# Four edits to a hybrid GLA + RWKV-7 step: fewer x rows in waiting, state transposes ahead of projections, head sums as two fp32r products, and VectorE block transposes in place of TensorE's

## The chip, the cores and the metric

The kernel runs on one core of a Trainium2 chip. The metric is device microseconds (us) of one execution; lower is better. A few runs of the same kernel are shown by their median, and one further execution was recorded by the hardware profiler. The engines are called as the profile calls them: PE (TensorE matmuls), PEld (its weight loads), DVE (VectorE), ACT (ScalarE), POOL (GpSimd), SP (SyncE, which issues all DMAs here).

## The reference, cut to what matters

One layer of a decoder step, all in float32: 1024 prompt tokens and 8 sample tokens (with states of their own) go through one projection, two parallel recurrent branches, a gated merge and a layer norm.

```python
p = jnp.einsum('btd,dn->btn', x, w_in)                 # 1024 -> 3088 + 4224 + 2048 columns
q, k, v, g_a, a_lr = _split(p_gla, GLA_SPLITS)         # GLA: 4 heads, key 128, value 256
...
pr = p_rwkv + (prev - p_rwkv) * rwkv_mu                # token shift
r, kb, vb, g_b, w_lr, aa_lr = _split(pr, RWKV_SPLITS)  # RWKV-7: 16 heads of 64
kk = hr(kb * rwkv_k_k)
kk = kk / jnp.maximum(jnp.sqrt(jnp.sum(jnp.square(kk), axis=-1, keepdims=True)), L2_EPS)
...
# per token: S = S*w + (S·(-kk)) (kk*a)^T + v k^T ;  y = S r
y, S_rwkv = _rwkv7_scan(rh, hr(w), kh, vh, kk, hr(a), S_rwkv0)
mu = jnp.mean(y, axis=-1, keepdims=True)               # group norm per head
var = jnp.mean(jnp.square(y - mu), axis=-1, keepdims=True)
bonus = jnp.sum(rh * kh * rwkv_r_k, axis=-1, keepdims=True) * vh
...
m = sigmoid(gate_a) * (o_gla @ w_up_gla) + sigmoid(gate_b) * (o_rwkv @ w_up_rwkv)
y_out = _layernorm(DEEPNORM_ALPHA * x + m @ w_out, ln_g, ln_b, LN_EPS)
```

The outputs are the two y, and the new GLA, RWKV and shift states of both groups. Four sums over a head's 64 channels are taken per pair of heads: the one under `kk`, the one in `bonus`, and the mean and the variance of the group norm.

## The kernel before, in words

**Tiling.** Channels lie on the 128 partitions and tokens along the free dimension. The tokens go in two passes (`PASS`): pass 0 holds 512 prompt tokens and the 8 samples (two matmul tiles of 260), pass 1 the other 512. A block of the projection is 128 output columns: 8 steps over the 1024 inputs, and in each step three products of fp32r operands, `xh*whi`, `xl*whi`, `xh*wlo`, where hi is the value rounded to fp32r and lo is the rest. Per pass there are 73 blocks for `w_in`, then 8 for each of the two up projections, then the output projection. A weight row is split into hi and lo in pass 0, stored, and loaded again in pass 1.

**Order.** The kernel has no fixed loop order. Each piece of work is a Python generator (a stream) that yields one operation at a time; `Order.run` keeps a modelled time per engine, takes in each round the stream whose operation would start first, and issues it. Where two could start at the same time, a bonus by the kind of stream decides: `PRIO` on all engines but PE, `ON_PE` on PE. The projection blocks are one stream of kind "block" with bonus 0.0. The issued order is fixed when the kernel is built; on the chip each engine takes its instructions strictly in that order and waits at semaphores. Operations written through `self.C` may go to ACT or DVE, those through `self.E` to DVE or POOL, whichever ends first by the model.

**Buffers.** Tiles come from counted pools, and a stream that finds none waits: 26 `row` tiles of [128, 520], 4 `wide` of [128, 1024], 2 `part` (fp32r, for hi and lo of a sum's operand), 1 `sto`; in PSUM 2 banks `proj`, 3 `big`, 1 `pch`, 2 `pY`. The three `big` banks serve nearly everything beside the projections and the recurrent chain.

**A pair of RWKV heads** is one stream (`pair`), 8 pairs per pass, 16 in all. `front` makes decayed keys and values and the chunk matrices G (with two calls of `head_sums`), inverts 32x32 blocks by 31 DVE steps on the tiles `X` and `Xt`, with round trips through DRAM (`LD`, `XD`); `back` finishes the 64x64 inverses; `turn` makes the keys `BK` and the values `v` token-major; `chain` runs over the 8 chunks of 64 tokens one after the other, and a pair's chain starts only when the chain of the pair before has ended; `norm` (two more calls of `head_sums`) finishes. In pass 1 `chain` spawns `state`, a stream of kind "state" that takes a `big` bank, transposes the final state `Sp` on PE, copies it to `sto` and stores it (`rwkv_p`). The samples' streams (`rwkv_sample`, `tails`) are of kind "state" too.

**Head sums** are one float32 matmul of a [128, 512] row with a block matrix of ones (`heads`, part of the constants `cons`). **`turn`** transposes 8 chunks of `BK` [128, 128] and 4 blocks of `v` on PE through three `big` banks and copies them back: 2 copies of 128x512 and 4 of 64x256 per pair. The tile `L` of the inversion is used again for the values.

**`load_x`** loads the 8 rows of the next matmul's moving operand (x, the branch outputs or the merged rows) into `row` tiles; two helper streams split each into `xh` and `xl`, for which there is one buffer per step, free only when the last block that reads the old one is done. `swap` starts it 3 blocks early (`AHEAD`). For x itself, `low_rank` also multiplies the raw rows, three at a time.

Of the kernel before, what the change touches and what calls it, by code (L numbers as in the profile page):

```python
# [11 lines left out]
F32R = mybir.dt.float32r  # L12
# [8 lines left out]
P = 128  # L21
# [5 lines left out]
HT = TP // 2  # L27

PASS = [(0, HT + NS, NS, [(0, 260), (260, 260)]), (HT + NS, HT, 0, [(0, 512)])]
GH, GDK, GDV = 4, 128, 256  # L30
RH, RN = 16, 64
NPAIR = RH // 2
C = 64
NCH = HT // C
# [21 lines left out]

KEEP = 1
AHEAD = 3
SPARE_ROWS = 8


# [12 lines left out]
PRIO = {"evacuate": 0.7, "pair": 0.4, "turn": 0.5, "chain": 0.5, "norm": 0.1, "x": 0.7, "lora": 0.2, "rank": -0.3,  # L74
        "head": 0.3, "gate": 0.05, "w": 0.3, "out": -0.1, "state": 0, "block": 0.0}
ON_PE = {"evacuate": 0.0, "pair": 0.15, "turn": 0.1, "chain": 0.15, "norm": 0.15, "x": 0.0, "lora": 0.15, "rank": 0.1,
         "head": 0.1, "gate": 0.06, "w": 0.0, "out": -0.03, "state": 0.0, "block": 0.0}

URGENT = 0.6
SIGMOID, EXP = "sigmoid_and_others", "natural_log_exp_and_others"  # L80
# [2 lines left out]
HS = (slice(0, 64), slice(64, 128))  # L83
# [7 lines left out]

CST = {}
_o = 0
for _n, _w in [("ident", 128), ("gmask", 256), ("heads", 128)]:
    CST[_n] = (_o, _w)
    _o += _w
CST_W = _o
# [9 lines left out]
def constants():  # L107
    c = np.zeros((P, CST_W), np.float32)

    def put(name, v):  # L110
        o, w = CST[name]
        c[:, o:o + w] = v

    i = np.arange(P)
    put("ident", np.eye(P))
    put("heads", (i[:, None] // C) == (i[None] // C))
    s, t = i[:, None] % C, i[None, :] % C
    put("gmask", np.concatenate([s < t, s <= t], axis=1))
    lev = np.zeros((P, 64 * MASKED), np.float32)
    for n, m in enumerate(LEVELS[:MASKED]):  # L120
        ri = np.array([x for x in range(P) if (x // m) % 2 == 1])
        j = i[:, None]
        lev[:, 64 * n:64 * n + 64] = ((j // (2 * m)) == (ri[None, :] // (2 * m))) & ((j // m) % 2 == 0)
    return c, lev


class Op:
# [274 lines left out]
class Kern(Order):  # L402
# [57 lines left out]

    def head_sums(self, x):

        ps = yield from self.bank("big", [P, HT])
        yield self.P.matmul(ps, self.cst("heads"), x, start=True, stop=True)
        return ps

    def pvec(self, name, j):
# [4 lines left out]
    def setup(self):  # L472
        nc, a = self.nc, self.a
        E = mybir.EngineType
        self.es.enter_context(self.tc.manual_schedule(engines={E.PE, E.Activation, E.DVE, E.Pool, E.SP}))
        cp = self.pool("const")
        wp = self.pool("w", side="left")
        self.dr = self.pool("dr", space=DRAM)
        pp = self.pool("psum", space=PSUM)
        xp = self.pool("x", side="right")  # L480
        self.r1 = r1 = self.pool("work", side="left")
        for tag, bufs in BANKS.items():
            self.buffers(tag, bufs, lambda tag=tag, bufs=bufs: pp.tile([P, 512], F32, name=tag, bufs=bufs))
        for tag, (shape, bufs) in SBUF.items():
            dt = F32R if tag in PARTS else F32
            self.buffers(tag, bufs, lambda tag=tag, shape=shape, bufs=bufs, dt=dt:
                         r1.tile(shape, dt, name=tag, bufs=bufs))
        for tag, (shape, bufs) in WBUF.items():
            dt = F32 if tag == "wraw" else F32R
            self.buffers(tag, bufs, lambda tag=tag, shape=shape, bufs=bufs, dt=dt:  # L490
                         wp.tile(shape, dt, name=tag, bufs=bufs))
        for k in range(NK):
            for v in "hl":
                tag = f"x{v}{k}"
                self.buffers(tag, 1, lambda tag=tag: xp.tile([P, HALF], F32R, name=tag, bufs=1))
        nc.scalar.preload_act_table_set(EXP)
        self.cons = cp.tile([P, CST_W], F32, name="cons")
        self.pv = cp.tile([P, PV_W], F32, name="pv")
        self.ident = self.cst("ident")
        self.omu = cp.tile([P, NRC], F32, name="omu")  # L500
        self.oka = cp.tile([P, 8], F32, name="oka")
        self.nkk = cp.tile([P, 8], F32, name="nkk")
        self.bias = {}
        for n, v in [("glaeps", GLA_EPS), ("gneps", GN_EPS), ("lneps", LN_EPS), ("one", 1.0),
                     ("kkl", 0.5 * math.log(KK_SCALE))]:
            t = cp.tile([P, 1], F32, name="b_" + n)
            nc.vector.memset(t, v)
            self.bias[n] = t
        dbg = getattr(self, "dbg", {})
        self.o_gla = dbg.get("o_gla", None) or self.dr.tile([D, T], F32, name="o_gla")  # L510
        self.o_rwkv = dbg.get("o_rwkv", None) or self.dr.tile([D, T], F32, name="o_rwkv")
        self.sg = [[[self.dr.tile([P, PASS[i][1]], F32, name=f"sg{i}{n}{k}") for k in range(NK)] for n in range(2)]
                   for i in range(2)]
        self.mg = [[self.dr.tile([P, PASS[i][1]], F32, name=f"mg{i}{k}") for k in range(NK)] for i in range(2)]

        self.lev = cp.tile([P, 64 * MASKED], F32, name="lev")

        self.onesr = cp.tile([P, P], F32R, name="onesr")
        self.wa = cp.tile([P, NK * 16], F32, name="wa")
        self.alr = [cp.tile([96, HALF], F32R, name=f"alr{n}") for n in range(2)]  # L520
        self.gw2 = cp.tile([96, GH * GDK], F32R, name="gw2")
        self.GS = [cp.tile([P, GDV], F32, name=f"GS{h}") for h in range(GH)]

        self.smp = cp.tile([P, 4, NPAIR, NS], F32, name="smp")
        self.RS = self.dr.tile([4, NS, D], F32, name="RS")
        self.WA = self.dr.tile([2, NS, D], F32, name="WA")
        self.tail = cp.tile([P, NS + 1, NRC], F32, name="tail")
        self.carry = cp.tile([P, NRC], F32, name="carry")
        self.shT = cp.tile([P, NRC, NS], F32, name="shT")
        self.reset = cp.tile([P, HT], U8, name="reset")  # L530
        nc.vector.memset(self.reset, 1)
        nc.vector.memset(self.reset[:, ::C], 0)

        self.Sp = [cp.tile([P, C], F32, name=f"Sp{n}") for n in range(NPAIR)]
        for t in self.Sp:
            nc.gpsimd.memset(t, 0.0)

        for tag, n, bufs in (("az", 4 * HT, 2), ("XT", 2 * HT, 2), ("X1", HT, 1), ("As", 2 * HT, 1)):
            ts = [cp.tile([P, n], F32, name=f"{tag}{i}") for i in range(bufs)]
            for t in ts:  # L540
                nc.gpsimd.memset(t, 0.0)
            self.fixed(tag, ts)
# [9 lines left out]
    def load_constants(self):  # L552
        a, V, E = self.a, self.V, self.E
        yield from self.load("wa", self.S.dma_start(self.wa, a["wa"]))
        self.has.add("wa")
        row = yield from self.row()
# [13 lines left out]
        yield V.tensor_scalar(self.nkk, self.pv[:, o:o + 8], -1.0, None, ALU.mult)  # L570
        self.has.add("pv")
        yield from self.load("cst", self.S.dma_start(self.cons, a["cst"]))
        raw = row[0:96, :GH * GDK]
        for n in range(3):
            yield self.S.dma_start(raw[32 * n:32 * n + 16], a["gla_alpha_w2"])
        yield self.S.dma_start(self.lev, a["lev"])
        yield V.tensor_copy(self.gw2, raw)
        yield V.tensor_sub(self.gw2[64:96], raw[64:96], self.gw2[64:96].bitcast(F32))
        self.free(row)
        self.has.add("cst")  # L580


    def load_x(self, src, i, wait=None, low_rank=False):
# [3 lines left out]
        base, n = PASS[i][:2]  # L587
        raws, his, xs, used = [], [], [], [NK]
# [20 lines left out]
        self.spawn(high(), "x")  # L609
        self.spawn(low(), "x")  # L610
        for k in range(NK):
            raw = yield from self.row(n)
            rows = slice(k * P, (k + 1) * P)
            yield from self.load(f"x{k}", self.S.dma_start(
                raw, src[k] if isinstance(src, list) else src[rows, base:base + n]))
            raws.append(raw)
# [540 lines left out]

    def turn(self, d):

        for x in range(0, NCH, 4):  # L1160
            pt = yield from self.bank("big", [P, 4, P])
            for n in range(4):
                yield self.tr(pt[:, n], d.BK[:, x + n])
            yield self.C.copy(d.BK[:, x:x + 4], pt)
            self.free(pt)
        d.u = d.L.rearrange("p (c h v) -> p c h v", c=NCH, h=2)
        pt = yield from self.bank("big", [P, 4, P])
        for n in range(4):
            yield self.tr(pt[:, n], d.v[:, n * P:(n + 1) * P])
        self.free(d.v)  # L1170
        for h in range(2):
            for n, hs in enumerate(HS):
                yield self.C.copy(d.u[HS[1 - h], n::2, h], pt[hs, :, h * C:h * C + C])
        self.free(pt)

    def chain(self, c, p, d):
        A, V = self.A, self.V
# [335 lines left out]
    def swap(self, src, i, wait=None, low_rank=False):  # L1513

        if self.plan:
            self.plan[-1].last = True
        self.todo = (max(0, len(self.plan) - AHEAD), (src, i, wait, low_rank))

# [94 lines left out]

def layout(i):
    f = np.ascontiguousarray
    cst, lev = constants()
    ch = lambda v: v.reshape(-1, P).T
    pv = np.concatenate([ch(i["rwkv_mu"][0]), ch(i["rwkv_w0"][0]), ch(i["rwkv_a0"][0]), ch(i["rwkv_k_k"][0]),
                         ch(i["rwkv_k_a"][0]), ch(i["rwkv_r_k"][0].reshape(-1)), ch(i["rwkv_lnx_w"][0]),
# [2 lines left out]
    x = np.concatenate([xp, xs], axis=0)  # L1622
    xT = f(np.concatenate([xp[:HT], xs, xp[HT:]], axis=0).T)
    return {
        "cst": cst, "lev": lev, "pv": f(pv), "xT": xT, "x": f(x), "w_in": f(i["w_in"][0]),
        "wa": f(i["w_in"][0][:, OFF_A:OFF_R].reshape(NK, P, 16).transpose(1, 0, 2).reshape(P, NK * 16)),
        "gla_alpha_w2": f(i["gla_alpha_w2"][0]), "state_gla": f(i["state_gla"]), "state_rwkv": f(i["state_rwkv"]),
        "shiftT": f(i["state_rwkv_shift"][0].reshape(NS, NRC, P).transpose(2, 1, 0)),
# [25 lines left out]
```

## Time and profile before

| | |
|---|---|
| median of 3 runs | 1686.61 us (1685.98 to 1691.09) |
| profiled execution | 1687.94 us, span of the trace 1686.2 us |
| granted TensorE clock, mean | 0.986 |
| busy share PE / PEld / DVE / ACT / POOL | 97% / 85% / 70% / 49% / 5% |
| DMA | 315.26 MB, 187 GB/s over the span |

A busy PE is not a PE at its peak: a matmul's record includes the time until its result lands, so the records of neighbours overlap (a 128x512 fp32r product has a record of 0.40 us and starts 0.23 us after the one before). The granted clock of a stretch stands as PEclk. Nearly all instructions are recorded under one line, L214, the helper that issues them; groups are therefore told apart by their tiles.

### The profile page before, as it was taken

The page shows a single profiled execution, that of the slowest core. Times are in us where ns is not written, and L with a number is a line of the kernel's source. Part 1 is how long each engine was busy: PE and PEld are TensorE (multiplying, and loading weights), DVE is VectorE, ACT ScalarE, POOL GpSimd, SP SyncE. Part 2 cuts the span into 40 slices and gives each one's busy share as a digit, 9 for nine tenths or more (in the row PEclk, how much of TensorE's full clock was granted, in tenths as well). Part 3 has the DMA queues.
Part 4 walks back from the last instruction along what each step waited for, and adds up shares of the span by engine and source line. Part 5 has one row for each costly group of instructions (what it writes and reads, how often), then busy time and mean ns, then how long its engine had stood idle before and what let it go on. Part 6 is the DMA issues. An engine that isn't in the chain of part 4 may idle for free.

```text
span 1686.2 us, 29927 instructions
## 1 busy us (share of the span) xinstructions
PE 1628.7 (97%) x10322; PEld 1430.9 (85%) x10322; DVE 1184.6 (70%) x3114; ACT 830.7 (49%) x1974; POOL 86.0 (5%) x183
## 2 busy tenths in 40 slices
PE   8999999999999998999999999999989999999998
PEld 7899999999999996888878778778867889988786
DVE  6777876887688766757656477898728876656565
ACT  5456755664657465443634254526243656644210
POOL 1100000100000000000000000200000000000000
PEclk9999999999999999899999999999988999999999
DMA  9777675777587657545364625454642487788522
GB/s 291 246 228 231 217 215 152 227 246 218 160 245 228 216 158 237 170 119 174 101 206 123 186 73 176 152 163 156 202 145 67 114 275 221 236 278 278 182 78 87
DMA packets 311778, 315.26 MB, mean 187 GB/s; under 512 B 75347, under 2 KB 197084, under 8 KB 311628
## 3 DMA queue, kind: packets, MB, share of 16 engines
q1 hardware_dynamic: 311628, 313.36, 59.9%
q8 instruction: 82, 1.34, 0.3%
q14 instruction: 68, 0.56, 0.1%
HBM read 195.45 MB, written 117.82 MB: 186 GB/s over the span
## 4 chain that ended last, share of the span: by engine, by line
PE 73%; DVE 12%; DMA 7%; ACT 3%; issue 2%; SPq 2%; POOL 0%; POOLq 0%; DVEq 0%; ACTq 0%
PE proj L214 41%; PE big L214 21%; PE pY L214 7%; DVE row L214 4%; PE pch L214 4%; DMA wide<-LD 2%; SPq L214 2%; DVE X L214 2%; DVE Xt L214 2%; ACT row L214 1%; DVE wide L214 1%; DMA row<-state_rwkv 1%; DVE wlo L214 1%; DVE az L214 1%; DMA wraw<-w_up_gla 1%
## 5 line engine op out<-in xcount | busy, mean ns | idle before, releaser
L214 PE MATMUL proj<-xl,whi 128*128 128x260 f32 (+1 forms) x1928 | 637.5, 331 | 0.0
L214 PE MATMUL proj<-xh,whi 128*128 128x260 f32 (+1 forms) x1928 | 635.9, 330 | 0.0
L214 PE MATMUL proj<-xh,wlo 128*128 128x260 f32 (+1 forms) x1928 | 635.0, 329 | 0.0
L214 PEld LDWEIGHTS proj<-xh,wlo 128*128 128x128 f32 x1928 | 364.9, 189 | 29.9 <-issue 6.6
L214 PEld LDWEIGHTS proj<-xh,whi 128*128 128x128 f32 x1928 | 365.2, 189 | 28.5 <-issue 5.4
L214 PEld LDWEIGHTS proj<-xl,whi 128*128 128x128 f32 x1928 | 364.9, 189 | 28.6 <-issue 6.5
L214 DVE TENSOR_TENSOR row<-row 128x256 f32<-128x256 f32 (+6 forms) x326 | 161.7, 503 | 23.8 <-ACT row L214 11.8
L214 ACT CAST whi<-wraw 128x512 fp32r<-128x512 f32 x210 | 129.9, 622 | 95.7 <-PE proj L214 51.7
L214 DVE TENSOR_TENSOR wlo<-wraw,whi 128x512 fp32r<-128x512 f32 x205 | 141.0, 691 | 40.5 <-ACT whi L214 37.3
L214 ACT ACTIVATE row<-row 128x512 f32<-128x512 f32 (+4 forms) x229 | 138.4, 611 | 44.6 <-DVE row L214 26.3
L214 DVE TENSOR_TENSOR Xt<-X,wide 128x60 f32<-128x60 f32 (+24 forms) x496 | 105.4, 212 | 43.8 <-DMA wide<-LD 31.2
L214 ACT ACTIVATE row<-proj,omu 128x260 f32<-128x260 f32 (+1 forms) x99 | 54.1, 547 | 150.2 <-PE proj L214 149.9
L214 PE MATMUL big<-row 128*128 128x64 f32 (+4 forms) x712 | 115.6, 282 | 12.5 <-DVE row L214 11.5
L214 PEld LDWEIGHTS big<-row 128*128 128x128 f32 (+1 forms) x712 | 96.9, 193 | 23.3 <-DVE row L214 13.5
L214 ACT ACTIVATE s0p<-wide,pc 64x64 f32<-64x64 f32 x256 | 88.1, 344 | 52.7 <-DVE wide L214 48.5
L214 DVE TENSOR_TENSOR X<-X,Xt 128x60 f32<-128x60 f32 (+24 forms) x496 | 104.8, 211 | 11.9
L214 ACT COPY wide<-pch 64x64 f32<-64x64 f32 x221 | 45.5, 206 | 114.3 <-PE pch L214 110.4
L214 DVE SCALAR_TENSOR_TENSOR row<-proj,pv,row 128x259 f32<-128x259 f32 (+1 forms) x99 | 56.3, 569 | 49.7 <-ACT tail L214 33.7
L214 DVE SCALAR_TENSOR_TENSOR wide<-pch,pc,s0p 64x64 f32<-64x64 f32 x224 | 63.1, 282 | 38.3 <-PE pch L214 33.7
L214 POOL TENSOR_TENSOR row<-row 128x512 f32<-128x512 f32 (+7 forms) x43 | 45.5, 1059 | 794.4 <-ACT row L214 211.7
L214 ACT COPY row<-big 128x128 f32<-128x128 f32 (+7 forms) x165 | 46.7, 307 | 66.8 <-PE big L214 63.5
L381 ACT ACT_TABLE_LOAD x56 | 71.8, 1283 | 1.0
(254 smaller groups left out, 2560.6 us busy)
## 6 DMA issues: line engine op xcount, KB each, us to landing
wraw<-w_in SPq DMA_DIRECT2D x146, 256.0 KB
wh<-whi SPq DMA_DIRECT2D x146, 256.0 KB
wl<-wlo SPq DMA_DIRECT2D x146, 256.0 KB
whi<-wh SPq DMA_DIRECT2D x146, 256.0 KB
wlo<-wl SPq DMA_DIRECT2D x146, 256.0 KB
wide<-LD SPq DMA_DIRECT2D x64, 128.0 KB
wraw<-w_up_gla SPq DMA_DIRECT2D x32, 256.0 KB
wraw<-w_up_rwkv SPq DMA_DIRECT2D x32, 256.0 KB
```

The costliest lines, as they stand in the source:

```text
L214: ways.append((eng, lambda call=call: call(out, *args, **kw), price(eng, name, out, args, ins)))
L381: self.nc.scalar.preload_act_table_set(self.table)
```

## The change

Four edits, independent of each other in the code:

1. `load_x`: the load of row k is held back until fewer than 4 loaded rows wait for their split (`RAWS`), except for the first x.
2. `ON_PE["state"]` goes from 0.0 to 0.1, so that PE operations of the "state" streams are taken ahead of projection products that could start at the same time.
3. `head_sums`: the operand is split into hi and lo (one rounding copy on ACT or DVE, one subtraction on DVE or POOL), and two fp32r products with an fp32r block matrix `headsr` are summed in PSUM in place of one float32 product. The block matrix is loaded by a DMA of its own and cast once.
4. `turn`: no PE transposes. DVE transposes the 32x32 blocks of `BK` (into `L`) and of `v` (into a new `row`), and 16 + 8 copies of [32 partitions x 256], on ACT or DVE, put the blocks in their places. `L` is freed after the copies, and the values take another `wide` tile.

```diff
+RAWS = 4
...
-         "head": 0.1, "gate": 0.06, "w": 0.0, "out": -0.03, "state": 0.0, "block": 0.0}
+         "head": 0.1, "gate": 0.06, "w": 0.0, "out": -0.03, "state": 0.1, "block": 0.0}
...
     def head_sums(self, x):
 
+        hi, lo = yield from self.split(x)
         ps = yield from self.bank("big", [P, HT])
-        yield self.P.matmul(ps, self.cst("heads"), x, start=True, stop=True)
+        yield from self.sums(ps, self.headsr, hi, lo)
+        self.free(hi, lo)
         return ps
...
+        self.headsr = cp.tile([P, P], F32R, name="headsr")
...
-        raw = row[0:96, :GH * GDK]
+        raw, heads = row[0:96, :GH * GDK], (yield from self.row(P))
+        yield self.S.dma_start(heads, a["heads"])
...
+        yield V.tensor_copy(self.headsr, heads)
...
         for k in range(NK):
+            yield lambda: k - len(his) < RAWS or low_rank and not i
             raw = yield from self.row(n)
...
     def turn(self, d):
 
-        for x in range(0, NCH, 4):
-            pt = yield from self.bank("big", [P, 4, P])
-            for n in range(4):
-                yield self.tr(pt[:, n], d.BK[:, x + n])
-            yield self.C.copy(d.BK[:, x:x + 4], pt)
-            self.free(pt)
-        d.u = d.L.rearrange("p (c h v) -> p c h v", c=NCH, h=2)
-        pt = yield from self.bank("big", [P, 4, P])
-        for n in range(4):
-            yield self.tr(pt[:, n], d.v[:, n * P:(n + 1) * P])
+        q = [slice(32 * n, 32 * n + 32) for n in range(4)]
+        t, tv_ = d.L.rearrange("p (c j f) -> p c j f", c=NCH, j=4), (yield from self.row(HT))
+        yield self.V.transpose(d.L, d.BK.rearrange("p c t -> p (c t)"))
+        yield self.V.transpose(tv_, d.v[:, :HT])
         self.free(d.v)
+        for i in range(4):
+            for j in range(4):
+                yield self.C.copy(d.BK[q[j], :, q[i]], t[q[i], :, j])
+        self.free(d.L)
+        u = yield from self.get("wide")
+        d.u = u.rearrange("p (c h v) -> p c h v", c=NCH, h=2)
+        tv = tv_.rearrange("p (c j f) -> p c j f", c=NCH, j=2)
         for h in range(2):
-            for n, hs in enumerate(HS):
-                yield self.C.copy(d.u[HS[1 - h], n::2, h], pt[hs, :, h * C:h * C + C])
-        self.free(pt)
+            for i in range(2):
+                for j in range(2):
+                    yield self.C.copy(d.u[q[2 - 2 * h + j], :, h, q[i]], tv[q[2 * h + i], :, j])
+        self.free(tv_)
```

More of the change, by code (lines that the diff above doesn't have):

```diff
@@ L93 @@
 _o = 0
-for _n, _w in [("ident", 128), ("gmask", 256), ("heads", 128)]:
+for _n, _w in [("ident", 128), ("gmask", 256)]:
     CST[_n] = (_o, _w)
@@ L115, in constants @@
     put("ident", np.eye(P))
-    put("heads", (i[:, None] // C) == (i[None] // C))
     s, t = i[:, None] % C, i[None, :] % C
@@ L123, in constants @@
         lev[:, 64 * n:64 * n + 64] = ((j // (2 * m)) == (ri[None, :] // (2 * m))) & ((j // m) % 2 == 0)
-    return c, lev
+    return c, lev, ((i[:, None] // C) == (i[None] // C)).astype(np.float32)
 class Op:
@@ L578, in load_constants @@
         yield V.tensor_sub(self.gw2[64:96], raw[64:96], self.gw2[64:96].bitcast(F32))
-        self.free(row)
+        yield V.tensor_copy(self.headsr, heads)
+        self.free(row, heads)
         self.has.add("cst")
@@ L1615, in layout @@
     f = np.ascontiguousarray
-    cst, lev = constants()
+    cst, lev, heads = constants()
     ch = lambda v: v.reshape(-1, P).T
@@ L1624, in layout @@
     return {
-        "cst": cst, "lev": lev, "pv": f(pv), "xT": xT, "x": f(x), "w_in": f(i["w_in"][0]),
+        "cst": cst, "lev": lev, "heads": heads, "pv": f(pv), "xT": xT, "x": f(x), "w_in": f(i["w_in"][0]),
         "wa": f(i["w_in"][0][:, OFF_A:OFF_R].reshape(NK, P, 16).transpose(1, 0, 2).reshape(P, NK * 16)),
```

## The prediction

> **What bounds the kernel now.** I read the page's busy shares first, then what PE waits for, then stage windows (us of PE, PEld, DVE, ACT, POOL, then granted clock, DMA share, GB/s), then the chain that ended last and PE's timeline where the windows looked odd.
>
> ```profile
> PE 1628.7 (97%) x10322; PEld 1430.9 (85%) x10322; DVE 1184.6 (70%) x3114; ACT 830.7 (49%) x1974; POOL 86.0 (5%) x183
> PE big L214 <- DVE row L214: 13.4, 11, 5.5
> PE pch L214 <- DVE rh L214: 6.5, 10, 1.4
> 0.00:1391.00 1391.00, 1345.60 (x8731) 1187.68 (x8732) 1010.14 (x2799) 721.48 (x1759) 83.25 (x180) 0.98 0.60 185
> 1391.00:1686.00 295.00, 283.08 (x1593) 243.23 (x1592) 174.46 (x316) 109.25 (x215) 2.77 (x3) 0.99 0.60 194
> ```
>
> PE is busy 97%, and its longest sum of waits on one releaser is 13.4 us: PE bounds the kernel nearly everywhere, so work taken off PE should show. The second row of windows is the tail of up and output projections. All pairs' DVE work but little is in the first 1391 us, where DVE is at 1010.14/1391 = 73%.
>
> ```profile
> 632.00:716.00 84.00, 76.44 (x468) 64.35 (x467) 59.90 (x155) 42.66 (x97) 3.92 (x13) 0.92 0.66 205
> 935.00:1000.00 65.00, 59.78 (x288) 48.59 (x286) 37.13 (x89) 24.52 (x56) 4.00 (x9) 0.92 0.44 130
> 1000.00:1188.00 188.00, 183.78 (x1004) 153.22 (x1004) 154.75 (x409) 90.91 (x225) 20.58 (x28) 1.00 0.51 157
> 1238.00:1306.00 68.00, 59.21 (x302) 47.46 (x300) 44.67 (x128) 29.75 (x79) 2.99 (x9) 0.85 0.26 74
> ```
>
> Three stretches of pass 1 lose PE time, in gaps and by a lowered clock; 1000:1188 beside them shows the usual state (2.2% idle, clock 1.00). Ahead of two of them the chain of waits has nothing but projections for 27 and 50 us:
>
> ```profile
> 935.08 27.42 PE proj L214 x118
> 1187.97 50.17 PE proj L214 x216
> 1188.00:1238.00 50.00, 0.04 (x1) 0.15 (x2) 0.69 (x1) 0.00 (x0) 1.00 0.73 226
> 1237.96 0.49 PE L214 MATMUL big<-cons,Sp 128*64 128x128 f32 x3
> L214 PE MATMUL big<-cons,Sp x8: 270/271/273, 962.4 to 1579.7; 128*64 128x128 f32 x8
> ```
>
> The third row counts only operations on `big` banks: none in 50 us of pass 1. What ends it is three transposes of `Sp` in a row. `state` takes its bank before it asks for PE, and its bonus of 0.0 ties with the projections, which are in the list before it; so three finished pairs sit on all three `big` banks, and front, back, turn, norm and GLA can't get one until the projections run dry. When the banks come free, PE has few projections left to fill with, and the gaps follow.
>
> **The clock.** The wait of 5.5 us is at 670.7, and the clock behind it is 0.50:
>
> ```profile
> 676.22 1.02 PE L214 MATMUL big<-row 128*128 128x8 f32 x4 [5.49 <-DVE row L214]
> 678.00:682.00 4.00, 3.13 (x14) 2.94 (x15) 3.62 (x16) 0.26 (x3) 0.00 (x0) 0.50 0.30 102
> 1241.00:1245.00 4.00, 3.07 (x14) 2.74 (x14) 0.83 (x2) 0.97 (x3) 0.00 (x0) 0.70 0.21 67
> 1245.00:1249.00 4.00, 2.39 (x11) 1.80 (x10) 0.69 (x1) 2.67 (x5) 0.00 (x0) 0.50 0.00 0
> ```
>
> So a gap costs itself and some microseconds at half clock behind it. The Trainium skill, "TensorE: Matmul & The Clock Gate", section "Part 1: The HAM clock gate", says that an idle window of about 3.4 us halves the clock; the first two rows agree, while in the last two PE is idle 0.9 and 1.6 us of 4 and the clock falls all the same, so density counts as well as the longest gap.
>
> **Part 1: head sums.** 16 pairs x 4 = 64.
>
> ```profile
> 730.62 1.02 PE L214 MATMUL big<-row,cons 128*128 128x512 f32 x2
> L214 PE MATMUL big<-row,cons x128: 590/592/1167, 47.9 to 1461.4; 128*128 128x512 f32 x128
> 700.83 0.40 PE L214 MATMUL proj<-xl,whi 128*128 128x512 f32 x1
> 701.06 0.40 PE L214 MATMUL proj<-xh,wlo 128*128 128x512 f32 x1
> L214 DVE CAST part<-row x5: 420/426/429, 683.9 to 1319.0; 128x512 fp32r<-128x512 f32 x4, 128x520 fp32r<-128x520 f32 x1
> L214 ACT CAST part<-row x5: 615/628/642, 172.9 to 1561.3; 128x520 fp32r<-128x520 f32 x3, 128x512 fp32r<-128x512 f32 x2
> L214 DVE TENSOR_TENSOR part<-row,part x8: 684/690/694, 174.4 to 1319.7; 128x520 fp32r<-128x520 f32 x4, 128x512 fp32r<-128x512 f32 x4
> ```
>
> A float32 product is two records (128 for 64); the pair spans 1.02, one lasts 0.59, so the second starts 0.43 after the first, and a head sum holds PE for 0.86 us. fp32r products follow each other by 0.23, so two hold it for 0.46. PE: 64 x 0.40 = -25.6 us. Added: 64 casts (0.43 on DVE or 0.63 on ACT) and 64 subtractions (0.69 on DVE), and about 1.2 us of latency per sum inside a pair's stream.
>
> **Part 2: turn.** 12 PE transposes per pair, 192 in all.
>
> ```profile
> 717.38 0.60 PE L214 MATMUL big<-cons,wide 128*128 128x128 f32 x4
> 717.82 0.60 PE L214 MATMUL big<-cons,row 128*128 128x128 f32 x4
> L214 ACT COPY wide<-big 64x256 f32<-64x256 f32 x61 | 22.4, 367 | 3.5 <-PE big L214 2.2 <-DVE wide L214 0.5
> L214 ACT COPY wide<-big 128x512 f32<-128x512 f32 x27 | 15.8, 586 | 11.5 <-PE big L214 11.2
> L214 DVE STREAM_TRANSPOSE row<-row 128x512 f32<-128x512 f32 x16 | 11.3, 704 | 0.0
> L214 DVE CAST l2p<-l2s x12: 284/294/296, 44.0 to 1318.8; 128x256 fp32r<-128x256 f32 x12
> L214 ACT CAST l2p<-l2s x4: 405/406/426, 117.1 to 813.6; 128x256 fp32r<-128x256 f32 x4
> ```
>
> Four transposes take 0.44, so 0.11 each: PE -192 x 0.11 = -21.1 us. Removed on ACT (mostly): 2 x 0.59 + 4 x 0.37 = 2.6 us per pair. Added on DVE: one transpose of 512 (0.70) and one of 1024 (twice, 1.41): 2.1. Added on either: 24 copies of 256 elements a partition. No row has them with 32 partitions from SBUF; the casts of 256 are nearest, 0.29 on DVE and 0.41 on ACT. Bounds: all on DVE 24 x 0.29 = 7.1 us per pair, all on ACT 9.8. The turn gets some 5 us longer; PE fills with projections meanwhile, so I cost that latency at nothing in the sum; for the last pair the cover is the up projections, and if the cover is gone it is 5 us per pair (fourth rival).
>
> The Trainium skill speaks against this part: "VectorE: DVE Perf Modes", section "Rules for kernel authors", sends a 128x128 transpose to TensorE where PSUM will do. In engine time the rows agree with it: 12 x 0.11 + 2.6 = 3.9 us before against 9 to 12 us after. It would be the better way if PE had room, and PE has none; how that could turn the sign is the third rival.
>
> **Part 3: state transposes first.** The eight transposes cost the same; the banks come free at once. At stake are 65 - 59.78 = 5.2 and 68 - 59.21 = 8.8 us of gaps, and 8% of 65 and 15% of 68 = 15.4 us of clock: up to -29. The usual 2.2% idle stays (-3), and the refilled order has waits of its own; I take -20, between 0 (the banks are held by others then) and -26. By the code SP gains too: a store that waits for the one `sto` tile holds up all issues behind it, and three no longer come at once.
>
> **Part 4: few x rows.**
>
> ```profile
> 651.05 2.46 SPq L214 DMA_DIRECT2D row<-xT  x5
> L214 ACT CAST xh<-row x8: 613/617/624, 693.4 to 697.1; 128x512 fp32r<-128x512 f32 x8
> 2.11 4.32 DMA row<-xT
> ```
>
> Pass 1's eight rows are issued by 655 and split only at 693: 8 of 26 rows lie idle 40 us. Four come free, which can help the stretch 632:716 (7.6 us of gaps, 8% of clock: at most -14); but its 5.49 us wait is a sample matmul behind a DMA, not a missing row, so I take 0. The cost: a swap's fifth row may be issued late. A flight of 4.3 us against four steps of three products (4 x 0.69 = 2.8) leaves 1.5 us, over the 7 later swaps at most +11; I take 0, since a row issued in time has its 3 blocks of lead as before. On SP the issues only move later. The `heads` DMA at the start takes 64 KB that `cons` loses: 0.
>
> **What DVE and ACT pay.** Per pair DVE gets 2.1 + 4 x 0.69 = 4.9 us for certain (78 us in all), and up to 4 x 0.43 + 7.1 = 8.8 more (219 in all, if nothing goes to ACT). With PE's 46.7 us and the 20 of part 3 gone, the first 1391 us become 1324, and DVE's share 1088/1324 = 82% to 1229/1324 = 93%. How full can DVE be with PE still fed?
>
> ```profile
> 505.00:548.00 43.00, 42.93 (x345) 41.33 (x345) 37.26 (x93) 31.88 (x75) 1.42 (x2) 1.00 0.73 229
> 1096.00:1138.00 42.00, 39.91 (x222) 33.31 (x221) 38.21 (x115) 11.73 (x32) 1.91 (x2) 1.00 0.54 163
> ```
>
> At 87% PE was full; at 91% it lost 2 us in 42. The middle (1159 us) is at 87.5%, just there. If 87% is the ceiling, the middle costs 1159/0.87 - 1324 = +8, the upper end +89. ACT has room (52% there), and the model sends copies to it when DVE is late, so I stay near the middle and take +20, with 0 and +89 as ends.
>
> **The sum**, against the profiled execution (1687.94, which is 1686.2 of span and 1.7 around it): -25.6 - 21.1 - 20 + 0 + 20 = -46.7, so 1641. The median shown is 1.3 lower: 1640.
>
> **The rivals.**
> - All of it lands: -25.6 - 21.1 - 26 - 14, no DVE cost: 1601. For it: ACT half idle, POOL idle. Against: DVE at 82% at best.
> - The banks were not the cause, or the stall moves: the "state" bonus gives 0, and the rest stays: 1661. Against: the three `Sp` in a row end it.
> - Slower, by one mechanism: DVE becomes the bound in the pair stage. DVE takes all 24 copies and casts, 1229 us, and can't be kept above 87%: 1413 us of stage against 1391, +22, so 1709. It turns the sign where the ceiling is under 1229/1391 = 88%. For it: the copies change partition block each time, and the rows above lose PE time at 91%. Against: the planner counts DVE's time and can use ACT.
> - PE's time comes back as waits: the order is made anew, the streams in it are serial, and a quarter of the 10 us of added latency per pair (5 in turn, 4 x 1.2 in the sums) shows as PE gaps with half clock behind them: 16 x 2.5 = +40, 1681. For it: the 5.5 us wait shows that the planner's times can be off. Against: PE's waits inside the chain are short now (6.5 us in 10).
>
> **How the numbers follow.** Sum 0.45 (own range 1622 to 1658), all lands 0.18, banks not the cause 0.12, given back 0.13, DVE-bound 0.12. From no change a measurement can tell about 0.3%, 5 us, so 1682 to 1692 is "same". Faster: 0.45 + 0.18 + 0.12 + 0.05 of the "given back" = 0.80; same 0.07; slower 0.13. The range leaves out the slow case and the edge of the fast one: 1603 to 1690.
>
> **What would show it.** Right: no `Sp` transposes in threes, no 50 us of pure projections, the clock above 0.99; `big<-part,headsr` records of 0.39 instead of 0.59; PE's matmul count down by 192; DVE busy 1260 to 1400 with PE still at 96%. Wrong: PE under 93% with long waits on DVE block copies (`wide<-wide`), block copies far above 0.3 us, or new gaps of over 3 us with 0.50 behind them. At swaps, waits of PE on `row<-xT`, `row<-o_gla` or `row<-mg` would show part 4 as a cost.

## The result, and the profile after

The changed kernel takes 1634.97 us (median of four runs, 1634.04 to 1635.56); the kernel before takes 1687.66 us (four runs, 1685.98 to 1691.09). The ratio is 0.9685, with a 95% interval of 0.9668 to 0.9702, so 52.7 us are gained where 46.7 were forecast. The profiled execution took 1634.97 us with a span of 1633.0.

First the busy shares and the clock by slices, from the page of the changed kernel, then its two stage windows (us of PE, PEld, DVE, ACT, POOL, then granted clock, DMA share, GB/s):

```profile
PE 1580.9 (97%) x10130; PEld 1404.8 (86%) x10130; DVE 1309.8 (80%) x3396; ACT 880.3 (54%) x2112; POOL 116.0 (7%) x204
PEclk9999999899999999999999999999999999999999
```

```profile
0.00:1391.00 1391.00, 1347.86 (x8935) 1208.97 (x8936) 1165.45 (x3153) 799.98 (x1960) 111.98 (x200) 0.99 0.63 194
1391.00:1633.00 242.00, 233.01 (x1197) 195.79 (x1196) 144.30 (x244) 80.31 (x152) 4.06 (x4) 0.99 0.58 188
```

The matmul count is down by 192, DVE is up by 125 us, and PE is still busy 97%. Only one slice of the 40, that from 286 to 327 us, has a clock under 0.9. Both first windows end at 1391 us, so the gain shows in the second row: pass 1 has got further by then, and the tail is 242 us instead of 295.

A split of the span that is used throughout: idle PE time (span less busy), clock loss (one less the granted clock, times the span), and the rest, which is PE's work at full clock. Idle time at half clock is counted in both of the first two, so the three are good to a few us only. Before it is 57.5 + 23.6 + 1605; after, 52.1 + 18.0 + 1563. PE's work fell by 42 us, idle time by 5, clock loss by 6.

The stretches that the prediction showed of before, in the changed kernel:

```profile
632.00:716.00 84.00, 78.79 (x446) 63.28 (x445) 62.69 (x164) 45.16 (x107) 8.98 (x17) 0.94 0.66 209
935.00:1000.00 65.00, 63.75 (x346) 53.24 (x346) 58.33 (x114) 37.52 (x92) 12.83 (x14) 1.00 0.53 160
1000.00:1188.00 188.00, 178.75 (x922) 146.42 (x921) 168.76 (x456) 82.99 (x203) 22.83 (x30) 1.00 0.54 167
1238.00:1306.00 68.00, 67.98 (x400) 58.11 (x399) 52.94 (x145) 44.92 (x115) 7.81 (x11) 1.00 0.46 141
```

The second and the fourth have nearly no gap left and the full clock. The first still loses 5.2 us in gaps and 6% of the clock: from 640 to 650 us PE is busy 5.90 us at a clock of 0.77, with DVE busy 9.59 (before: PE 9.36 us at 1.00). The third, the "usual state" of before, now idles 9.25 us instead of 4.2. The transposes of `Sp` and the longest pieces of projections in the chain that ended last:

```profile
L215 PE MATMUL big<-cons,Sp x8: 270/271/272, 842.3 to 1410.3; 128*64 128x128 f32 x8
```

```profile
13.62 19.57 PE proj L215 x160
844.41 18.12 PE proj L215 x78
```

The first `Sp` is transposed at 842 instead of 962, one at a time, and no piece of pure projections is longer than 20 us, where there was one of 50.

The groups that the change added, kept apart by shape (line, engine, operation, out<-in, shapes, count | busy us, mean ns of one | idle us ahead and what ended it), and two head-sum products among projections in the timeline:

```profile
L215 ACT COPY wide<-wide 32x256 f32<-32x256 f32 x181 | 73.0, 403 | 18.1 <-DVE wide L215 16.0
L215 DVE TENSOR_TENSOR part<-row,part 128x512 fp32r<-128x512 f32 x62 | 44.0, 710 | 3.4 <-ACT part L215 2.3
L215 DVE COPY wide<-row 32x256 f32<-32x256 f32 x97 | 29.7, 306 | 1.5
L215 DVE COPY wide<-wide 32x256 f32<-32x256 f32 x75 | 22.5, 300 | 1.3
L215 DVE STREAM_TRANSPOSE row<-row 128x512 f32<-128x512 f32 x32 | 22.0, 688 | 0.2
L215 DVE STREAM_TRANSPOSE wide<-wide 128x1024 f32<-128x1024 f32 x16 | 19.9, 1245 | 0.2
L215 ACT COPY wide<-row 32x256 f32<-32x256 f32 x31 | 12.5, 403 | 0.4
```

```profile
706.00 0.40 PE L215 MATMUL big<-part,headsr 128*128 128x512 f32 x1
706.24 0.39 PE L215 MATMUL proj<-xl,whi 128*128 128x512 f32 x1
```

ACT took 212 of the 384 block copies at 0.40 us, DVE 172 at 0.30. In the place shown, a head-sum product holds PE for 0.24 us.

And what is new and bad: one wait of PE. These are the timeline and the windows of the changed kernel around it:

```profile
289.17 1.69 DVE L215 SCALAR_TENSOR_TENSOR row<-row 128x512 f32<-128x512 f32 x1
...
296.25 0.62 ACT L215 CAST part<-row 128x512 fp32r<-128x512 f32 x1 [5.34 <-DVE row L215]
...
296.92 0.80 PE L215 MATMUL big<-part,headsr 128*128 128x512 f32 x1 [8.47 <-ACT part L215]
```

```profile
290.00:294.00 4.00, 0.00 (x0) 0.00 (x0) 3.97 (x7) 0.91 (x2) 0.32 (x1) 0.55 0.11 43
294.00:298.00 4.00, 1.08 (x4) 0.85 (x4) 3.97 (x8) 1.55 (x3) 0.12 (x1) 0.50 0.02 1
298.00:302.00 4.00, 4.00 (x15) 3.54 (x15) 3.97 (x5) 0.25 (x1) 2.23 (x6) 0.50 0.95 287
286.00:302.00 16.00, 7.53 (x39) 6.64 (x38) 15.80 (x24) 6.65 (x13) 3.62 (x7) 0.64 0.51 161
```

PE waits for a rounding copy on ACT, ACT for a row from DVE, and DVE is full: 15.80 of 16 us. So the chain of a head sum has become the wait, 8.5 us long, and PE's first 4 us of full work behind it run at half clock.

### The profile page after: what moved, and what is told of

Same layout as the page of the kernel before. It is cut to its first block, busy times and chain, and to the rows that moved or that the text cites. A ratio compares the mean times of both kernels' runs of the same rounds, so it can differ in the third digit from the quotient of the medians.

```text
span 1633.0 us, 29970 instructions
## 1 busy us (share of the span) xinstructions
PE 1580.9 (97%) x10130; PEld 1404.8 (86%) x10130; DVE 1309.8 (80%) x3396; ACT 880.3 (54%) x2112; POOL 116.0 (7%) x204
## 4 chain that ended last, share of the span: by engine, by line
PE 73%; DVE 14%; DMA 6%; ACT 4%; issue 2%; SPq 1%; POOL 0%; DVEq 0%; POOLq 0%; ACTq 0%
PE proj L215 41%; PE big L215 20%; PE pY L215 7%; PE pch L215 4%; DVE row L215 4%; DVE wide L215 2%; DMA wide<-LD 2%; ACT row L215 1%; DVE X L215 1%; SPq L215 1%; DVE az L215 1%; DMA wraw<-w_in 1%; DVE wlo L215 1%; DVE Xt L215 1%; ACT wide L215 1%
## 5 line engine op out<-in xcount | busy, mean ns | idle before, releaser
L215 PE MATMUL proj<-xh,whi 128*128 128x260 f32 (+1 forms) x1880 | 618.2, 329 | 1.1 <-DVE row L215 0.7
L215 PE MATMUL proj<-xl,whi 128*128 128x260 f32 (+1 forms) x1880 | 617.6, 328 | 0.2 <-DVE xl L215 0.2
L215 PE MATMUL proj<-xh,wlo 128*128 128x260 f32 (+1 forms) x1880 | 616.6, 328 | 0.7 <-POOL wlo L215 0.5
L215 PEld LDWEIGHTS proj<-xh,whi 128*128 128x128 f32 x1880 | 356.6, 190 | 28.5 <-issue 2.6
L215 PEld LDWEIGHTS proj<-xh,wlo 128*128 128x128 f32 x1880 | 356.2, 189 | 26.3 <-issue 2.1
L215 PEld LDWEIGHTS proj<-xl,whi 128*128 128x128 f32 x1880 | 356.4, 190 | 24.8 <-issue 2.6
L215 ACT CAST whi<-wraw 128x512 fp32r<-128x512 f32 x210 | 129.1, 620 | 81.4 <-PE proj L215 34.7
L215 DVE TENSOR_TENSOR row<-row 128x512 f32<-128x512 f32 (+9 forms) x317 | 158.7, 504 | 7.7 <-ACT row L215 3.0
L215 ACT ACTIVATE row<-row 128x512 f32<-128x512 f32 (+5 forms) x229 | 138.3, 611 | 32.5 <-DVE row L215 17.6
L215 POOL TENSOR_TENSOR row<-row 128x512 f32<-128x512 f32 (+7 forms) x52 | 60.0, 1156 | 560.8 <-DVE row L215 204.5
L215 ACT COPY wide<-wide 32x256 f32<-32x256 f32 x181 | 73.0, 403 | 18.1 <-DVE wide L215 16.0
L215 DVE SCALAR_TENSOR_TENSOR wide<-pch,pc,s0p 64x64 f32<-64x64 f32 x224 | 63.0, 281 | 21.1 <-PE pch L215 16.8
```

The source lines that it names most:

```text
L215: ways.append((eng, lambda call=call: call(out, *args, **kw), price(eng, name, out, args, ins)))
```

## The experiments

Each time is a median, and each ratio is to the kernel before on the same chip, with its 95% interval. Differences between two changed kernels are taken from the medians; from the ratios they come out up to 3 us higher or lower. The theory was the prediction's: the savings of PE time and the freed banks add up, and the few rows do nothing. The rival was that the parts depend on each other: that a saving of PE time comes back as waits where something else holds the pairs up, and that the edits of order decide how much.

### What holds the banks

The theory of part 3: finished pairs sit on the `big` banks. The prediction showed three transposes of `Sp` at the end of the stall at 1238 us. At the end of the other, at 962 us, there are only two of them (from 962.42); the third transpose that had waited is one of the samples' tile `smp`:

```profile
L214 PE MATMUL big<-cons,smp x2: 270/272/273, 962.3 to 985.1; 128*128 128x128 f32 x2
```

So the samples' stream, of the same kind "state", takes its bank before it asks for PE just as `state` does, and is one of the holders. Three kernels, each made from the kernel before. `only_state` makes edit 2 alone. `bank_keep` leaves all bonuses alone, and lets `state` take a bank only when all three are free. `bank_sample` does the same, and gives the samples' stream, alone, the bonus 0.1.

```diff
 # only_state
-  "out": -0.03, "state": 0.0, "block": 0.0}
+  "out": -0.03, "state": 0.1, "block": 0.0}
 # bank_keep
-        pt = yield from self.bank("big", [C, P])
+        pt = (yield from self.get("big", 1, 2))[:C, :P]
 # bank_sample: as bank_keep, and in ON_PE
+  "state": 0.0, "sample": 0.1, "block": 0.0}
-        self.spawn(samples(), "state")
+        self.spawn(samples(), "sample")
```

> The kernel before with the bonus of the state streams alone. Theory A (PE bounds, the parts add up): the stalls on the three big banks go, ratio 0.988 (-20 us; 0.983 to 1.000), Sp transposes one by one, no 50 us of pure projections, mean clock above 0.99. Rival B (the banks are held by others, the stall moves): ratio 0.997 to 1.003 and the long runs of projections remain. Rival C (any change makes a new order, and orders differ by some 10 us by luck): any ratio between 0.993 and 1.007, with new gaps at other places.

> The kernel before, bonus unchanged at 0.0, but a state stream of pass 1 takes its big bank only when all three are idle, so that two are never held by it. If the held banks were the cause (theory A), this alone does what the bonus does: ratio 0.988, no 50 us of pure projections, though the Sp transposes still come late. If the place of the transposes on PE matters and not the banks (rival), the ratio is 0.997 to 1.003.

> The kernel before; the states of pass 1 keep the bonus 0.0 but take a big bank only when all three are idle, and the samples' stream gets the bonus 0.1. In the run with the bank rule alone there was no gap from 700 to 1400, but the samples' transposes came at 1343 instead of 962 and PE then sat idle for 80 us. If held banks made the stalls and the starved samples made that late gap, this kernel has neither: 1660 to 1670 like the bonus alone, ratio 0.983 to 0.989. If the late gap comes from the bank rule itself: above 1720.

Measured: `only_state` 1664.42 us, ratio 0.9864 [0.9847, 0.9881]; `bank_keep` 1753.41 us, 1.0388 [1.0373, 1.0403]; `bank_sample` 1666.61 us, 0.9880 [0.9866, 0.9893]. The first and the third are as expected. The second missed by 85 us and was the more instructive for it. Its windows of pass 1, those of `bank_sample`, then the first window in the kernel before:

```profile
700.00:1342.00 642.00, 633.27 (x3366) 524.37 (x3365) 420.60 (x1198) 299.71 (x710) 22.80 (x63) 1.00 0.49 149
...
1400.00:1500.00 100.00, 18.89 (x68) 11.94 (x66) 64.10 (x112) 24.04 (x53) 2.53 (x2) 0.53 0.33 98
```

```profile
700.00:1342.00 642.00, 631.21 (x3353) 521.58 (x3352) 464.04 (x1271) 304.03 (x721) 37.50 (x74) 1.00 0.50 155
...
1400.00:1500.00 100.00, 97.92 (x644) 88.54 (x643) 60.23 (x117) 53.00 (x100) 0.00 (x0) 1.00 0.81 258
```

```profile
700.00:1342.00 642.00, 619.60 (x3210) 509.87 (x3209) 444.70 (x1227) 283.30 (x675) 41.92 (x80) 0.98 0.48 147
```

Up to 1342 us `bank_keep` did what was expected of it: PE idles 8.7 us instead of 22.4, and the clock goes from 0.98 to 1.00. Then PE idles 81 us in one hundred, most of it in a single wait of 68.6 us for `row<-OS`, a load near the end of the samples' stream. The transposes of the samples' tile `smp` in both kernels, `bank_keep` first, tell why:

```profile
L214 PE MATMUL big<-cons,smp x2: 272/272/273, 1342.6 to 1349.5; 128*128 128x128 f32 x2
```

```profile
L214 PE MATMUL big<-cons,smp x2: 272/272/273, 839.3 to 843.4; 128*128 128x128 f32 x2
```

The samples' stream ties with the projections too, and with the banks never running dry nothing let it in until the projections ended; its serial work then lay bare at the end. With a bonus of its own its transposes are done at 843, and the time is that of `only_state` within 2.2 us, though the states of the pairs have no bonus. In both kernels the gaps from 700 to 1342 us are gone, once with the samples late and once with them early, so the held banks are shown to be the cause of the stalls. Edit 2 has a second effect that the prediction didn't see: it also brings the samples in, and takes them off a bank. How much of its gain is due to the samples alone is open; their bonus without the bank rule was not run.

### Each saving of PE time alone

`only_sums` and `only_turn` make edit 3 and edit 4 alone; `no_state` is the changed kernel with the bonus back at 0.0.

```diff
 # only_sums, from before
+        hi, lo = yield from self.split(x)
...
-        yield self.P.matmul(ps, self.cst("heads"), x, start=True, stop=True)
+        yield from self.sums(ps, self.headsr, hi, lo)
 # only_turn, from before
-                yield self.tr(pt[:, n], d.BK[:, x + n])
...
+        yield self.V.transpose(d.L, d.BK.rearrange("p c t -> p (c t)"))
...
 # no_state, from after
-  "out": -0.03, "state": 0.1, "block": 0.0}
+  "out": -0.03, "state": 0.0, "block": 0.0}
```

> The kernel before with the head sums in two fp32r products alone. Theory A: PE loses 64 x 0.40 = 25.6 us, DVE gains some 60 us spread over 1391, ratio 0.986 (0.983 to 0.990). Theory B (DVE is as much the bound as PE): less than half of it, ratio 0.993 to 1.0. Theory C (orders differ by luck): 0.979 to 0.993, with single gaps of several us in the trace.

> The kernel before with the small transposes and block copies alone. Theory A: PE loses 192 x 0.11 = 21 us, DVE gains some 70 us, ratio 0.989 (0.986 to 0.994). Theory B (DVE bound): 0.996 to 1.01. In this kernel the turn frees the big banks too, so it may also shorten the stalls on them: then up to 0.980.

> The changed kernel with the bonus of the state streams taken back. If the stall on the big banks is still there without the bonus (theory A, parts add): ratio to the kernel before 0.980 (20 us lost of the 53), Sp transposes in threes. If the turn without banks has made the stall harmless: 0.969 to 0.972.

Measured: `only_sums` 1703.97 us, 1.0091 [1.0068, 1.0114]; `only_turn` 1701.38 us, 1.0083 [1.0069, 1.0096]; `no_state` 1690.32 us, 1.0013 [1.0003, 1.0023]. `only_sums` and `no_state` lie outside all that was expected of them. `only_turn` lies in the range of its rival (DVE as the bound), but not by that mechanism, as the windows below show: DVE is busy 145.78 of 188 us where the loss is. Each saving alone costs some 14 us (15 and 14 by the ratios), and without the one number 0.1 the whole change is worth nothing. PE's work did fall, by the split above: idle + clock loss + rest is 71.3 + 35.6 + 1586 in `only_sums`, 81.4 + 40.8 + 1578 in `only_turn`, 79.1 + 50.7 + 1559 in `no_state`, against 57.5 + 23.6 + 1605. It was given back as gaps and half clock, and the windows show where. In each fence below the first row counts only operations on `big` banks, the second all work of the stretch in which the loss lies; the kernels are `no_state`, `only_turn`, `only_sums`.

```profile
970.00:980.00 10.00, 0.00 (x0) 0.00 (x0) 0.00 (x0) 0.00 (x0) 1.00 0.77 251
...
1000.00:1188.00 188.00, 164.74 (x843) 135.50 (x843) 165.52 (x433) 100.83 (x247) 15.71 (x28) 0.91 0.40 121
```

```profile
980.00:990.00 10.00, 0.00 (x0) 0.00 (x0) 0.00 (x0) 0.00 (x0) 1.00 0.54 180
...
1000.00:1188.00 188.00, 169.82 (x857) 137.80 (x855) 145.78 (x410) 94.08 (x226) 18.21 (x28) 0.93 0.42 126
```

```profile
1300.00:1310.00 10.00, 0.00 (x0) 0.00 (x0) 0.00 (x0) 0.00 (x0) 1.00 0.63 218
...
1306.00:1391.00 85.00, 73.39 (x360) 60.30 (x359) 49.82 (x121) 39.38 (x90) 3.37 (x8) 0.80 0.46 138
```

No bank is worked on while the projections run, then there is a stretch with gaps: 23.3 us of idle time and 9% of clock over 188 us in `no_state`, where the changed kernel loses 9.25 us and no clock. In all three, `Sp` is transposed two at a time where the pure projections end (at 990.7, 1016.8 and 1321.4), and just ahead of it stands a transpose of the samples' stream, of `smp` or of the row that came from `OS`. The timeline of `no_state`, then of `only_sums`:

```profile
990.63 0.27 PE L215 MATMUL big<-cons,smp 128*128 128x128 f32 x1
990.74 0.38 PE L215 MATMUL big<-cons,Sp 128*64 128x128 f32 x2
```

```profile
1321.15 0.27 PE L213 MATMUL big<-cons,row 64*128 64x64 f32 x1
```

It is the stall of the kernel before, and larger: idle time and clock loss are 40, 31 and 29 us in the stretches shown, against 10 and 19 in the two of before. That it grows because less PE work lies beside the pairs to fill with is argued from this; that the bonus removes it is shown.

### Each saving of PE time on top of the rest

`no_sums` is the changed kernel with the float32 head sums back, `no_turn` with the PE transposes back.

```diff
 # no_sums, from after
-        hi, lo = yield from self.split(x)
...
-        yield from self.sums(ps, self.headsr, hi, lo)
+        yield self.P.matmul(ps, self.cst("heads"), x, start=True, stop=True)
 # no_turn, from after
-        yield self.V.transpose(d.L, d.BK.rearrange("p c t -> p (c t)"))
...
+                yield self.tr(pt[:, n], d.BK[:, x + n])
```

> The changed kernel with the float32 head sums back. Theory A: 25.6 us of PE come back, ratio to the kernel before 0.983 to 0.985; the 8.5 us wait of PE on a head sum's cast goes. Theory B (DVE is the second bound): the sums were worth little on top of the turn, ratio 0.969 to 0.976.

> The changed kernel with PE's transposes back. Theory A: 21 us of PE come back, some 5 to 10 us of DVE pressure go, ratio to the kernel before 0.976 to 0.981. Theory B: 0.966 to 0.972, DVE share down from 80% to 76%.

Measured: `no_sums` 1651.63 us, 0.9792 [0.9770, 0.9814]; `no_turn` 1653.25 us, 0.9794 [0.9780, 0.9808]. The first lies between its two forecasts, the second is as theory A expected. So with the other three edits in place the sums are worth 16.7 us and the turn 18.3, where alone each cost about 14. PE's rest is 1587 and 1594 us in them, 24 and 31 above the changed kernel's 1563. Both run with fewer gaps than it (47.5 and 46.7 us idle, clock 0.994 and 0.993), which fits a price of the work on DVE. At the 8.5 us wait it can be seen directly; the stretch in `no_sums` and in `no_turn`:

```profile
286.00:302.00 16.00, 11.28 (x64) 9.42 (x63) 14.76 (x22) 7.93 (x18) 3.66 (x8) 0.89 0.31 98
```

```profile
286.00:302.00 16.00, 15.46 (x126) 14.96 (x126) 11.67 (x24) 15.16 (x38) 2.30 (x3) 1.00 0.39 118
```

PE idles 4.7 and 0.5 us there against 8.5 with both edits, and DVE is at 14.76 and 11.67 of 16 us against 15.80.

### The few x rows

`no_raws` is the changed kernel without the limit; `raws_pass1` limits only the loads of x for pass 1, and not those of the branch outputs and merged rows; `orders` is the kernel before with the bonus and the limit, and so with PE's work unchanged.

```diff
 # no_raws, from after
-            yield lambda: k - len(his) < RAWS or low_rank and not i
 # raws_pass1, from after
-            yield lambda: k - len(his) < RAWS or low_rank and not i
+            yield lambda: k - len(his) < RAWS or not (low_rank and i)
 # orders, from before
+            yield lambda: k - len(his) < RAWS or low_rank and not i
-  "out": -0.03, "state": 0.0, "block": 0.0}
+  "out": -0.03, "state": 0.1, "block": 0.0}
```

> The changed kernel without the limit on waiting x rows. I costed the limit at 0: ratio to the kernel before 0.967 to 0.970. If the four free rows matter at the change of pass: 0.972 to 0.978. If the limit costs at the swaps: 0.960 to 0.966.

> The kernel before with the two edits of order alone (state bonus, limit on x rows), PE's work unchanged. Theory D (the two edits of order remove two places where buffers are held; the PE savings only show once those places are gone): with the state bonus alone at 1664 and the limit worth about 14 us at the change of pass, 1645 to 1655, ratio 0.975 to 0.980, first xh cast of pass 1 near 680 instead of 693, and the PE savings are worth 15 to 20 us more in the full change. Rival E (the four edits only happen to fit together, orders differ by luck): 1660 to 1690, ratio 0.984 to 1.001, no common place.

> The changed kernel with the limit on waiting rows for the x of pass 1 alone; the loads of branch outputs and merged rows take all eight rows as before. Theory D says rows held at each such change cost where pairs still run: pass 1 starts at 678 as in the changed kernel, and the part lost near 1300 to 1400 (20 of the 33 us) comes back: 1648 to 1658, ratio 0.977 to 0.982. If only the change of pass matters: 1633 to 1640, ratio 0.968 to 0.972. Luck (E): anything up to 1670.

Measured: `no_raws` 1667.91 us, 0.9877 [0.9860, 0.9893]; `orders` 1659.39 us, 0.9838 [0.9824, 0.9851]; `raws_pass1` 1643.90 us, 0.9754 [0.9737, 0.9772]. None of the three came out as the theory had it: `no_raws` is worse than all that was expected, `orders` 4 us short of its range (and at the edge of the rival's), and `raws_pass1` lies between the theory's range and that for the change of pass alone. The limit that was costed at nothing is worth 32.9 us in the changed kernel: 24.0 from pass 1's x, 8.9 from the later loads (21 and 12 by the ratios). On top of the bonus alone it is worth only 5.0 (1664.42 to 1659.39). The pass change, in `no_raws` and in the changed kernel, by windows and then by the splits of x on ACT:

```profile
672.00:692.00 20.00, 13.78 (x76) 13.11 (x75) 14.79 (x59) 6.67 (x18) 1.36 (x1) 0.67 0.41 133
...
692.64 4.27 ACT L213 CAST xh<-row 128x512 fp32r<-128x512 f32 x8 [0.22 <-PE proj L213]
```

```profile
672.00:692.00 20.00, 20.00 (x113) 14.28 (x112) 16.51 (x54) 11.80 (x28) 1.84 (x1) 1.00 0.73 241
...
678.15 1.14 ACT L215 CAST xh<-row 128x512 fp32r<-128x512 f32 x2
```

Without the limit all eight rows are split together at 692.64, and the 20 us before lose 6.2 us of PE time and a third of the clock, 12.8 together. With it the first split stands at 678.15, the others follow one by one, and nothing is lost. That the projections get ahead because a block's result needs a `row`, of which x's eight hold a third, is argued from the code.

The other place is the last swaps. Windows of `no_raws`, `raws_pass1` and the changed kernel:

```profile
1320.00:1400.00 80.00, 70.81 (x469) 65.54 (x470) 56.73 (x155) 44.42 (x94) 3.16 (x7) 0.89 0.65 202
```

```profile
1320.00:1400.00 80.00, 70.57 (x534) 67.95 (x533) 55.60 (x157) 47.99 (x96) 1.26 (x1) 0.94 0.67 207
```

```profile
1320.00:1400.00 80.00, 76.79 (x616) 74.18 (x615) 58.03 (x160) 52.99 (x110) 1.29 (x1) 1.00 0.79 255
```

Idle and clock loss there are 18.0, 14.2 and 3.2 us. (The profiled execution of `raws_pass1` was its longest, 1649.82 us, so its row shows more loss than its median has.) Both places make 27.6 of the 34.8 us between the spans of `no_raws` and the changed kernel. In `orders` the pass change is mended as well (19.65 of 20 us busy at full clock, against 14.01 at 0.74 in `only_state`), but 1320 to 1400 us loses 7.0 us instead of 2.5: a part of the gain is given back there.

### A wider margin in the planner

The 8.5 us wait suggests that the planner places PE work too close behind DVE and ACT. `spare` doubles the slack that it adds to such results.

```diff
-SPARE = 0.4
+SPARE = 0.8
```

> The changed kernel with the planner's slack for PE behind another engine (SPARE) at 0.8 instead of 0.4 us, so that PE's dependent products are placed later and projections ahead of them. The changed kernel's largest gap (8.5 us at 288, behind a cast on ACT that waits for a full DVE, with half clock after it) should shrink: 1618 to 1632 if PE's remaining gaps come from products placed too early; 1635 to 1650 if the later placing costs the pairs as much as it saves.

Measured: 1650.33 us, 0.9790 [0.9776, 0.9804]: 15.4 us worse than the changed kernel. From 286 to 302 us it idles 6.6 us instead of 8.5, but by 1391 us PE was busy only 1338.87 us, against 1347.86. That is just past the poorer end of what was expected. The margin does not pay; how much of the 15 us is the margin and how much just another order is open. PE's work is the same in both kernels, so an order, with the choice of engines that goes with it, can make 15 us by itself, nearly as much as the head sums or the turn are worth.

## Why the prediction was right, and where not

The time (1640 forecast, 1635 measured) came true, and so did the mechanism of the likeliest case as far as PE's work and the freed banks go; but the four terms are not independent, and one of them was wrong. That the sum came within 6 us is in part luck: left out of the whole one at a time, the four edits are worth 16.7 + 18.3 + 55 + 32.9 = 123 us, while the whole gained 52.7.

- **PE's work.** Right: 42 us less, where 25.6 + 21.1 = 46.7 were computed, and the head-sum products follow by 0.24 us where 0.23 was taken.
- **State transposes.** The 20 us were right in isolation (23 measured), and the banks as cause are shown by `bank_keep` and `bank_sample`. In the whole change the step was mis-sized: without it 1690.32, with it 1634.97, so 55 us. The second rival priced a bonus without effect at 1661; the run without it says 1690. And the prediction had pairs alone on the banks, where the samples' stream held one of the three in all the stalls looked at but that at 1238 us.
- **DVE and ACT.** The block copies lie where the casts of 256 had put them (0.30 and 0.40 us for 0.29 and 0.41), and DVE's 125 us lie between 78 and 219, somewhat under the middle; the planner did send copies to ACT, as argued. The transpose of 1024 took 1.245 us, not 1.41. The 87% ceiling was not needed: DVE is at 84% in the first 1391 us. The +20 for DVE was about right in size, though what could be seen of it lies in single stretches where DVE is full (around 640 to 650 and 288 to 297 us) and not in an average: from `orders` (38.8 + 5.0 + 1613 by the split) to the changed kernel (52.1 + 18.0 + 1563), PE's work falls by 50 us, and idle time and clock loss grow by 26. The slower rival by DVE is refuted for this change: PE stays at 97%.
- **Few x rows.** Here the step failed: "its 5.49 us wait is a sample matmul behind a DMA, not a missing row, so I take 0". The row was read rightly and the conclusion was wrong: what lacked in that wait was other work for PE, and the limit brings pass 1's work forward by 15 us. The gain of at most 14 us, named and set aside, is there (12.8 at 672 to 692 us in the changed kernel). The feared cost at the swaps isn't: PE's waits on `row<-xT` are 5.1 us, all at the start (5.5 before), with none on `row<-o_gla` or `row<-mg`; the swaps gain 8.9 us.
- **Adding up.** The sum took the terms as independent. Along one path the sums come out: bonus and limit together give 28 us (20 forecast), then sums and turn together 24 us (46.7 less the 20 of DVE, so 26.7). Along the other path they don't: sums or turn first cost 14 us each. The rival "PE's time comes back as waits" was thus the outcome of three of the kernels, at 1690 to 1704, above its 1681; but it named added latency inside the pairs as the reason, and what the runs show is held banks. In the changed kernel it is kept out by the two edits of order, but for the 8.5 us at 288, a wait of the kind that was named as a sign of being wrong.
- **The signs.** No `Sp` in threes, no 50 us of projections, DVE at 1310 us (1260 to 1400) with PE at 97%: right. The clock is 0.989, just under the 0.99 that was named.

Open: which waits make up the loss of `only_turn` outside the stretch shown, and how far the order that the planner happens to find moves each of these times. The limit on x rows alone, and a kernel with more `row` tiles, which would test that shortage directly, were not run.

## What to carry to other kernels

Before taking work off the engine that bounds a kernel, look for streams that hold a scarce buffer (here a PSUM bank or a row) while they wait for a turn at low priority: the time saved can come back there as gaps with half clock behind them, and the saving measures as a loss. Try such edits both alone and left out of the whole; here the same edit cost 14 us one way and gained 18 the other, and neither number is its worth by itself. When a resource is given back earlier, ask who else stood behind the same priority: the samples, which held a bank themselves, were starved only once the stall that had let them in was gone.

## What the runs showed of the hardware

- The transpose of 128x1024 on DVE takes 1.245 us, 1.8 times the 0.688 of 128x512.
- A DVE operation on two rows of 128x512 took 1.69 us at 289.17, with a POOL operation on rows under way at the same time; its neighbours of the same shape take about 0.7. It is not the only one: in the trace of the changed kernel, of the DVE operations that the timeline lists one by one, some 120 overlap an arithmetic operation of POOL, and 29 of these took over 1.5 times the median of their own group; of some 2350 without such an overlap none did. (Groups of fewer than four, and the `COPY_PREDICATED` operations, which come in two lengths, are left out.)
- The clock was at 0.50 from 298 to 302 us although PE was busy all of these 4 us: it was still low from the gap before. So the 8.5 us of idle time cost at least 2 us more behind them (4 us at half clock). It fell early in the gap: PE's last product ended at 288.45 us, the mean clock was 0.60 from 290 to 292 and 0.50 from 292 on. Before, with the last product ending at 670.72, it was 1.00 from 671 to 672, 0.80 from 672 to 673 and then 0.50. So in both gaps the clock fell when about 2 us of them had passed. The prediction took its first two rows, a wait of 5.49 us and the low clock behind it, to agree with the idle window that it cites; the clock had fallen before a window of that length was over.
